# A Hymba layer on one core: segment decays from broadcast loads, a skip term taken before the scan, and another set of PSUM banks in attention

## The chip, the cores and the metric

The kernel runs one layer of a Hymba-style hybrid decoder on one core of a Trainium2 chip. The metric is the device time of one execution in microseconds (us), as the median of repeated runs. All data is float32.

## The reference, cut to what matters

A layer takes 1024 tokens and 16 learned meta tokens ahead of them (L = 1040 positions, model width 1024). One input projection feeds two mixers that stand side by side: a state-space mixer (SSD, 16 heads of 64 in two groups) and a stick-breaking attention (16 heads of 64). Their outputs go through one output projection, and a gated FFN with a short convolution follows. The change touches the two mixers:

```python
# SSD: chunks of 128 positions; the 16 meta tokens are a chunk of their own
xbc = silu(causal_dwconv(xbc, conv_w, conv_b))          # gives xs, Bm, Cm
dt  = softplus(dt_raw + dt_bias);  A = -exp(a_log)
Acs = cumsum(dt * A, axis=-1)                           # within a chunk, for each head
seg = Acs[..., :, None] - Acs[..., None, :]
Ldec = where(causal, exp(where(causal, seg, 0.0)), 0.0) # "segment decays"
CB  = einsum('bclgn,bcsgn->bgcls', Cc, Bc)
y_diag = einsum('bgcls,bgjcls,bcsgjp->bclgjp', CB, Ldec, Xdt)
states = einsum('bclgn,bgjcl,bclgjp->bcgjpn', Bc, exp(Acs[..., -1:] - Acs), Xdt)
# prev = states carried from chunk to chunk
y = y_diag + einsum('bclgn,bcgjpn,bgjcl->bclgjp', Cc, prev, exp(Acs))
y = y + xs * d_skip[:, None]                            # the "D term"
y = rms_norm(y.reshape(B, L, 1024) * silu(z), norm_g)

# stick-breaking attention, 128 queries at a time, strictly causal
zlog = q @ k.T / sqrt(64)
log_beta = log_sigmoid(zlog)
log_keep = where(valid, log_beta - zlog, 0.0)
after = cumsum(log_keep, reverse=True) - log_keep
o = where(valid, exp(log_beta + after), 0.0) @ v
```

## The kernel before

Products that need float32 accuracy are split: a number is held as a high and a low part in a type that TensorE (PE) multiplies faster, and hi·hi + lo·hi + hi·lo are added up in PSUM. VectorE is DVE, ScalarE is ACT, GpSimd is POOL, SyncE is SP; SP issues nearly all DMAs, in program order. PSUM has eight banks of 128 x 512 float32.

The program runs through these stages, one after the other (times in the profiled execution):

- **Head and projections, 0 to 448 us.** Norm, transposes, then the projections. Each feature block of `x` gets its convolution and silu on DVE and ACT (`conv_acts`, L485 to L510), is turned to tokens on PE and stored to DRAM as `xsd`; `dt_acts` (L605 to L668) makes dt, its hi and lo parts and three tables of decays, together six planes of `dtk`. The queries and keys of head pairs 0 to 3 are made here and stored to DRAM (`qkd`).
- **Scan, 448 to 621 us.** 18 units (group g, chunk c), L1021 to L1048; the two units of chunk 0 have 16 positions, the other 16 have 128. `chunk_weights` (L926) of the next unit is written ahead of `chunk_outputs` (L964) and `chunk_store` (L997) of this one. A unit makes the decays of its eight heads: ACT scales the triangle `tri` by dt·A's hi part eight times (`sgh`, L938), POOL does the lo part in one operation (`sgl`, L940), PE sums each along its columns (`sg`, four matmuls 512 wide, L947), ACT takes the exponential out of PSUM (`em`, L949). DVE multiplies by C·B (`cbm`, `em`, L953, L954). POOL makes `xdt` = x·dt (L957) and `yo` = x·D (L960). PE makes what the carried state gives (`yf`, L975), DVE scales it (`yt`, L977), POOL adds it to `yo` (L979). DVE makes `xw` (L983), PE the chunk's new state (`st`, L986), POOL and DVE the carried one (`pv`, L991, L994). PE gathers y in features by tokens: eight products of `em` and `xdt` (L1005), then `yo` added through a transpose (L1008). DVE multiplies by the gate (`zk`, L1012), ACT squares it (`sqk`, L1016).
- **Attention, 621 to 1032 us.** 8 head pairs p, each with 8 blocks i of 128 queries (`block_weights`, L1083): PE makes the logits `z` of up to three chunks of keys (L1101, two banks of PSUM to a tile, two tiles), ACT two sigmoids of each (`kp`, `bt`, L1102, L1103), DVE a reversed running product (`kp`, L1106), POOL the weights (`bt`, L1108). Some blocks later PE turns them to keys by queries (`tw`, L1120, in the same two tiles as `z`), ACT copies them out (`th`, L1122), and PE multiplies by v (`av`, L1135).
- **Rest of the first half of the output projection to 1079 us, its second half to 1172 us, FFN to 1831 us.** The change leaves these as they are, but for the size of the steps in which the output projection is handed out.

What sets the order. The projections of head pairs 4 to 7 (`pj_q`, `pj_k`: 32 chains of 24 matmuls of 246 or 260 columns) are not made ahead: they are **fill**, handed out in half chains by the generator `qk_fill` (L858) to keep PE at work in the scan and in attention; after them come the output projection's chains (`mo`, `out_steps`, L1283). A chain owns one of the two banks `mm` from its first matmul until ACT and DVE have taken it out (`st`, L864, L865). `SCAN_FILL` gives the half chains that go to the scan (30, and 4 ahead of it); the rest go to attention, the same number to each block (L1352, L1357). In attention the order of PE is the order in which the code is written (`pe_order`); the other engines, and PE in the scan, are ordered by a scheduler. `turn` is attention's queue: the transposes of a block begin once more than two blocks wait in it (L1367).

```python
        for p in range(8):                                  # L1356
            for i in range(NT):
                block = block_weights(p, i); next(block, None)   # z of two chunks of keys
                if mix: block_mix(*mix.pop(0))                   # av of an older block
                do(before)                                       # fill
                run(block)                                       # third chunk, then kp and bt
                if len(turn) > 2: ahead = begin_turn()           # tw and th of an older block
```

## Time and profile before

| what | value |
|---|---|
| median of 3 runs (lowest to highest) | 1831.24 us (1830.93 to 1832.59) |
| the profiled execution | 1833.03 us |
| its span, first to last instruction | 1831.3 us |
| TensorE clock granted, mean over the span | 0.974 of full speed |
| matmuls / all instructions | 11550 / 29209 |
| moved by DMA | 230.89 MB, 126 GB/s on average |

The page of the profile gives each engine's busy time and its share of the span, then the span in 40 slices in which a digit is the busy share in tenths; `PEclk` is the granted clock in the same way. A row of a window view gives, for a stretch of the span, its length, the busy time and number of instructions of PE, of PE's weight loads (PEld) and of the other engines, then the granted clock, the busy share of the DMA engines and their rate. A row of a view of groups gives line, engine, operation, output and inputs, shape, count, then the busy time, the mean of one in ns, and the engine's idle time just ahead of such instructions with what ended it. A row of a view of waits reads: who waited for whom, us in total, times, the longest.

### The profile page before, as it was taken

How to read it: one execution, taken by the hardware profiler on the slowest of the kernel's cores; microseconds unless marked ns; L12 is line 12 of the kernel's file. 1: busy time of each engine (PE TensorE's matmuls, PEld its weight loads, DVE VectorE, ACT ScalarE, POOL GpSimd, SP SyncE). 2: the span in 40 equal slices, each digit the busy share in tenths (PEclk: the TensorE clock that was granted, in tenths of full speed). 3: DMA queues.
4: the chain of work that ended last, by engine and by line, in shares of the span. 5: the costliest groups of instructions: out<-in, count | busy, mean ns of one | idle time of the engine just before them, and what ended most of it. 6: DMA issues, size and time to landing. Idle time of an engine off the chain costs nothing. (4 is left out here: it accounts for less than half of the span.)

```text
span 1831.3 us, 29209 instructions
## 1 busy us (share of the span) xinstructions
PE 1700.7 (93%) x11550; PEld 1465.1 (80%) x11550; DVE 1126.4 (62%) x1177; ACT 837.3 (46%) x1378; POOL 975.3 (53%) x687
## 2 busy tenths in 40 slices
PE   6899999999888888887789999999999999999998
PEld 5899999977666677675567778899889999888887
DVE  7755642453477666668555137766666666657777
ACT  6433333321455466676666334543333333334544
POOL 3655766321788677578667311267677677600001
PEclk9999999999799999998999999999999999999999
DMA  5233224335664332334211274323223333187335
GB/s 209 78 112 103 82 93 162 129 128 183 189 201 125 118 101 92 123 101 136 69 54 54 86 241 166 131 80 116 87 87 109 104 104 108 60 284 246 102 98 190
DMA packets 123144, 230.89 MB, mean 126 GB/s; under 512 B 13472, under 2 KB 55992, under 8 KB 122368
## 3 DMA queue, kind: packets, MB, share of 16 engines
q1 hardware_dynamic: 123008, 229.03, 38.4%
q8 instruction: 91, 1.49, 0.4%
q14 instruction: 45, 0.37, 0.1%
HBM read 151.31 MB, written 77.14 MB: 125 GB/s over the span
## 5 line engine op out<-in xcount | busy, mean ns | idle before, releaser
L1106 DVE TENSOR_TENSOR_SCAN kp<-kp,hold 128x272 f32<-128x272 f32 (+7 forms) x128 | 212.6, 1706 | 106.1 <-ACT kp L1102 32.3
L1108 POOL TENSOR_TENSOR bt<-bt,kp 128x256 f32<-128x256 f32 (+7 forms) x128 | 212.5, 1679 | 103.8 <-DVE kp L1106 89.5
L179 POOL TENSOR_TENSOR wlo<-wr,whi 128x1024 fp32r<-128x1024 f32 x43 | 99.3, 2318 | 40.3 <-ACT whi L178 40.3
L2093 POOL TENSOR_TENSOR fms<-fms 128x1 f32<-128x1 f32 x8 | 2.3, 289 | 221.9 <-ACT dh L1978 195.6
L1101 PE MATMUL z<-qk,qk 64*128 64x328 f32 (+8 forms) x672 | 80.7, 356 | 41.3 <-ACT th L1122 35.3
L1101 PEld LDWEIGHTS z<-qk,qk 64*128 64x128 f32 x672 | 52.9, 192 | 64.4 <-ACT th L1122 49.4
L1122 ACT ACTIVATE th<-tw 128x1024 f32<-128x1024 f32 (+2 forms) x96 | 75.2, 820 | 56.0 <-PE tw L1120 43.6
L1102 ACT ACTIVATE kp<-z 128x288 f32<-128x288 f32 (+6 forms) x112 | 83.0, 741 | 31.9 <-POOL cb L1109 17.7
L178 ACT ACTIVATE whi<-wr 128x1024 fp32r<-128x1024 f32 x43 | 45.7, 1064 | 110.9 <-PE fX L1644 67.5
L1120 PE MATMUL tw<-ident,bt 128*128 128x128 f32 x576 | 79.8, 281 | 15.5 <-ACT bt L1103 12.6
L1978 ACT ACTIVATE dh<-ar 128x512 fp32r<-128x512 f32 x77 | 48.7, 633 | 94.3 <-PE dnB L2056 44.7
L1716 DVE SCALAR_TENSOR_TENSOR ga<-gr,pp,ga 128x1024 f32<-128x1024 f32 x44 | 69.2, 1572 | 34.4 <-ACT ga L1709 33.6
L1120 PEld LDWEIGHTS tw<-ident,bt 128*128 128x128 f32 x576 | 65.4, 144 | 30.9 <-ACT bt L1103 15.6
L1135 PE MATMUL av<-th,v 128*64 128x128 f32 x1152 | 83.0, 292 | 0.3 <-ACT th L1122 0.3
L1103 ACT ACTIVATE bt<-z 128x288 f32<-128x288 f32 (+6 forms) x112 | 83.3, 743 | 0.0
L1979 DVE TENSOR_TENSOR dl<-ar,dh 128x512 fp32r<-128x512 f32 x77 | 53.2, 691 | 47.1 <-ACT dh L1978 47.1
L1135 PEld LDWEIGHTS av<-th,v 128*64 128x64 f32 x1152 | 66.6, 145 | 14.5 <-issue 12.1
L1777 POOL TENSOR_TENSOR al<-wr,ah 128x512 fp32r<-128x512 f32 x20 | 28.7, 1433 | 76.9 <-ACT ah L1776 76.8
L2056 PE MATMUL dnA<-dl,dh 128*128 128x512 f32 x176 | 68.5, 389 | 0.0
L2056 PE MATMUL dnA<-dh 128*128 128x512 f32 x176 | 68.5, 389 | 0.0
L2056 PE MATMUL dnA<-dh,dl 128*128 128x512 f32 x176 | 68.5, 389 | 0.0
L2056 PE MATMUL dnB<-dh 128*128 128x512 f32 x132 | 51.3, 389 | 0.0
(989 smaller groups left out, 6244.7 us busy)
## 6 DMA issues: line engine op xcount, KB each, us to landing
wr<-in_w_up SPq DMA_DIRECT2D x44, 512.0 KB
fds<-ga SPq DMA_DIRECT2D x44, 256.0 KB
b<-in_w_down SPq DMA_DIRECT2D x44, 256.0 KB
ar<-fds SPq DMA_DIRECT2D x44, 256.0 KB
fda<-ga SPq DMA_DIRECT2D x33, 256.0 KB
ar<-fda SPq DMA_DIRECT2D x33, 256.0 KB
qk<-qkd SPq DMA_DIRECT2D x16, 520.0 KB
qk<-qkd SPq DMA_DIRECT2D x16, 513.0 KB
```

The lines of the kernel that those rows point to most:

```text
L179: nc.gpsimd.tensor_tensor(l, raw, h.bitcast(F32), op=ALU.subtract)
L1101: mm(z[:, j, :w], u[h, :], r[h, a:a + w], start=s_ == 0, stop=s_ == 2)
L1102: nc.scalar.activation(kp[:, :, a:a + w], z[:, :, :w], AF.Sigmoid, scale=-QSCALE)
L1103: nc.scalar.activation(bt[:, :, a:a + w], z[:, :, :w], AF.Sigmoid, scale=QSCALE)
L1106: nc.vector.tensor_tensor_scan(kp[:, j][:, ::-1], kp[:, j][:, ::-1], hold[:, L - n:L][:, ::-1], 0.0, op0=ALU.mult, op1=ALU.max)
L1108: nc.gpsimd.tensor_tensor(bt[:, j, 0:m], bt[:, j, 0:m], kp[:, j, 1:m + 1], op=ALU.mult)
L1120: nc.tensor.transpose(tw[:, j, b, :], bt[:, j, c0:c0 + P], ident)
L1122: copied[0] = nc.scalar.activation(th[:, :, :nb, :], tw[:, :, :nb, :], AF.Copy).ins
L1135: mm(av[halves[j], :], v[:, kb, halves[j]], th[:, j, b, :], start=kb == 0, stop=kb == i)
L1716: nc.vector.scalar_tensor_tensor(v, self.g[jj][:, :, i:i + 256], fconv_w[:, j, i:i + 1], v, op0=ALU.mult, op1=ALU.add)
L1979: sub(lo[:, k], raw, hi[:, k].bitcast(F32), op=ALU.subtract)
L2056: mm(banks[BANK[n], t], u[:, 0, c], v[:, 1, :], start=(n in (1, 2, 5) and p == 0 and i == 0), stop=(p == NPR - 1 and i == 2), skip_group_c ...
```

## The change

In words, part by part:

1. **Segment decays.** `decay(0)` also copies the cumulative sums out of PSUM into `dtk[1]` (dt·A's hi and lo planes go; `dtk` has five planes). `turn_acs` turns them on PE (rows are chunk and head, columns positions), ACT copies them out and two DMAs store them to DRAM as `acsd`. Each unit loads its eight rows of 512 bytes to all 128 partitions (`load_bc`, 512 KB, two buffers, issued two units ahead). ACT makes relu(Acs[l] − row) eight times and one exponential of 128x1024 with scale −1. `sgh`, `sgl`, `sg` and `lowr` go.
2. **Multiplying by C·B** is cut in two: DVE takes six of the eight heads, POOL two.
3. **D term.** In the projection stage ACT scales each of the eight x blocks by D (128x1040) and SP stores it (`xdd`, 520 KB each). In the scan a unit loads 256 KB of it (`xd`); DVE adds it to y after PE, ahead of the gate. `yo` goes: both POOL operations, and the wait of the transposes for the second; they take `yt` from DVE.
4. **`xw`** moves from DVE to POOL.
5. **Fill.** Chains are handed out in quarters (6 matmuls). `SCAN_FILL` 30 becomes 36 half chains, and 8 half chains' worth of quarters is counted ahead of the scan where 4 half chains were, which are the same matmuls; so 6 half chains more are in the scan and 6 fewer in attention. In attention the rest is shared by the block's number in its pair (`FILL_AT`), few to the short blocks and more to the long ones, and in pieces between `z`, `av`, `tw`.
6. **Attention.** `zz` tiles 2 become 3 (six banks); the bank of `tp` goes, its users take a `zz` tile; `mm` has one bank in attention, two again behind it. `kp` buffers 2 become 3, `bt` 3 become 4, the queue begins its transposes one block later. k is loaded as one tile, q by blocks of 128 KB three blocks ahead; `qkd` holds both parts in one tensor.
7. **Output projection** steps are quarters too; `mo` is the same work.

```diff
-SCAN_FILL = 30
+SCAN_FILL = 36
+FILL_AT = (1, 1, 1, 4, 5, 6, 6, 6)
 def psum_mm(name):
-        return ps.tile([P, 512], F32, tag="mm", name=name, bufs=2)
+        return ps[0].tile([P, 512], F32, tag="mm", name=name, bufs=ps[1])
 def psum_zz(name):
-        return stage[0][1].tile([P, 2, 512], F32, tag="zz", name=name, bufs=2)
+        return stage[0][1].tile([P, 2, 512], F32, tag="zz", name=name, bufs=3)
 def plain_steps(...):
-                if halves_ and k == KB // 2:
-                    yield
+                if halves_ and k and k % halves_ == 0:
+                    yield 0
 def conv_acts(...):
+        def skip():
+            xd = raw[:, 0:L]
+            nc.scalar.activation(xd, box["d"], AF.Copy, scale=ssd_d[:, b:b + 1])
+            nc.sync.dma_start(out=xdd[b // 4][b % 4], in_=xd)
-        taps_ = [lambda j=j: tap(j) for j in range(4)] + [silu]
+        taps_ = [lambda j=j: tap(j) for j in range(4)] + [silu] + [skip] * (b < 8)
 def chunk_weights(g, c):
-            for h in range(8):
-                nc.scalar.activation(sgh[:nr, h, :nr], tri[:nr, :nr], AF.Copy,
-                                     scale=adh[:nr, c, 8 * g + h:8 * g + h + 1])
-            nc.gpsimd.tensor_tensor(sgl[:nr, :, :nr], tri..., adl..., op=ALU.mult)
-            for j in range(2):
-                pz = psum_z(f"sg{nm}_{j}").rearrange("p (a b) -> p a b", b=P)
-                for i, src in enumerate((sgh, sgl)):
-                    mm(pz[:nr, :, :nr], lowr[:nr, :nr], src[:nr, 4 * j:4 * j + 4, :nr], ...)
-                nc.scalar.activation(em[:nr, 4 * j:4 * j + 4, :nr], pz[:nr, :, :nr], AF.Exp)
+            for h in range(8):
+                nc.scalar.activation(em[:nr, h, :nr], bc[:nr, h, :nr], AF.Relu, scale=-1.0,
+                                     bias=acs[:nr, c, 8 * g + h:8 * g + h + 1])
+            nc.scalar.activation(em[:nr, :, :nr], em[:nr, :, :nr], AF.Exp, scale=-1.0)
...
-            nc.gpsimd.tensor_tensor(yo[:nr], xsc, dskip..., op=ALU.mult)
 def chunk_outputs(...):
+            nc.sync.dma_start(out=xd[:, :, y0:nr], in_=xdd[g][:, :, c0 + y0:c0 + nr]...)
-                nc.gpsimd.tensor_tensor(yo[:nr], yo[:nr], yt[:nr], op=ALU.add)
-                nc.vector.tensor_tensor(xw[:nr], xdt[:nr], dec..., op=ALU.mult)
+                nc.gpsimd.tensor_tensor(xw[:nr], xdt[:nr], dec..., op=ALU.mult)
 def chunk_store(...):
-            nc.vector.tensor_tensor(zk[:, :, ts], tp[:, :, ts], zk[:, :, ts], op=ALU.mult)
+            nc.vector.tensor_tensor(xd[:, :, ts], tp[:, :, ts], xd[:, :, ts], op=ALU.add)
+            nc.vector.tensor_tensor(zk[:, :, ts], xd[:, :, ts], zk[:, :, ts], op=ALU.mult)
 # attention
+    ps[:] = stage[0][1], 1
-        kpt = ap.tile([P, 2, L], F32, tag="kp", name=f"kp{nm}", bufs=2)
-        btt = ap.tile([P, 2, L], F32, tag="bt", name=f"bt{nm}", bufs=3)
+        kpt = ap.tile([P, 2, L], F32, tag="kp", name=f"kp{nm}", bufs=3)
+        btt = ap.tile([P, 2, L], F32, tag="bt", name=f"bt{nm}", bufs=4)
-            do(before)
-            run(block)
-            if len(turn) > 2:
-                ahead = begin_turn()
+        some(2)
+        run(block)
+        some(1)
+        if len(turn) > 3:
+            ahead = begin_turn()
+            some(1)
+        run(ahead)
+        some(9)
```

How the instructions move is seen best at three places. The rows of before and of the changed kernel stand apart; a row gives the line, the operation, the output and the inputs by the program's names, and the shape. First PE in the scan, between two units' pieces of fill (`yt` are the products that gather y and the transposes behind them, `sg` the sums of the segments, `pj_k`, `pj_q` fill):

```order
L215 MATMUL pj_k_1_260_5115<-b12rh,wl_k_4489 128x260
L1005 MATMUL yt_3_5128<-em_3_4991,xdt_3_5005 64x128 x8
L1008 MATMUL yt_3_5128<-ident,yo_3_5007 128x128 x4
L947 MATMUL sg_4_0_5159<-sgh_4_5147,lowr 128x512
L947 MATMUL sg_4_0_5159<-sgl_4_5148,lowr 128x512
L947 MATMUL sg_4_1_5163<-sgh_4_5147,lowr 128x512
L947 MATMUL sg_4_1_5163<-sgl_4_5148,lowr 128x512
L951 MATMUL cb_4_5167<-ct_4444,bt_4443 128x128
L215 MATMUL pj_k_1_260_5115<-b22h,wh_k_4488 128x260
```

The same place of the changed kernel:

```order
L217 MATMUL pj_q_0_0_5066<-b11h,wl_q_4754 128x246
L1024 MATMUL yt_3_5100<-em_3_4962,xdt_3_4978 64x128 x8
L1027 MATMUL yt_3_5100<-ident,yt_3_5079 128x128 x4
L217 MATMUL pj_q_0_0_5066<-b21h,wh_q_4753 128x246
L217 MATMUL pj_q_0_0_5066<-b21l,wh_q_4753 128x246
```

The four `sg` matmuls are gone from between the transposes and the fill, and the transposes take `yt` of DVE where they took `yo` of POOL.

Second, DVE in the scan, one unit (`em` is the multiplication by C·B, `zk` the gate, `xw` the state's input, `pv` the carried state), of before:

```order
L953 TENSOR_TENSOR cbm_3_5002<-cb_3_5000,tri 128x128
L954 TENSOR_TENSOR em_3_4991<-em_3_4991,cbm_3_5002 128x1024
L977 TENSOR_TENSOR yt_2_5013<-yf_2_5011,dtk_4439 128x512
L994 TENSOR_TENSOR pv_2_5020<-st_2_5018,pv_2_5020 128x512
```

and of the changed kernel, with the two operations that end a unit:

```order
L973 TENSOR_TENSOR cbm_4_5148<-cb_4_5146,tri 128x128
L884 TENSOR_TENSOR st_5130<-pj_q_0_0_5066,st_5130 128x246
L975 TENSOR_TENSOR em_4_5136<-em_4_5136,cbm_4_5148 128x768
L998 TENSOR_TENSOR yt_3_5169<-yf_3_5167,dtk_4448 128x512
L1014 TENSOR_TENSOR pv_3_5175<-st_3_5173,pv_3_5175 128x512
L1031 TENSOR_TENSOR xd_3_5165<-yt_3_5184,xd_3_5165 128x512
L1032 TENSOR_TENSOR zk_3_5163<-xd_3_5165,zk_3_5163 128x512
```

`em` of the next unit still stands ahead of `yt` of this one on DVE; it is a quarter shorter, `xd` stands ahead of `zk`, and `xw` is gone from DVE.

Third, PE in attention, where a chain of fill opens (`z` logits, `av` weights times v). Before:

```order
L1101 MATMUL z_4_1_7324<-qk_2_6687,qk_2_6681 128x328 x2
L1135 MATMUL av_1_7338<-th_1_0_7311,v_6847 64x128 x4
L215 MATMUL pj_q_0_260_7344<-b11h,wh_q_6654 128x260
L215 MATMUL pj_q_0_260_7344<-b11l,wh_q_6654 128x260
L215 MATMUL pj_q_0_260_7344<-b11h,wl_q_6655 128x260
```

After, the end of one chain and the start of the next:

```order
L217 MATMUL pj_k_1_260_6691<-b22h,wh_k_5779 128x260
L217 MATMUL pj_k_1_260_6691<-b22l,wh_k_5779 128x260
L217 MATMUL pj_k_1_260_6691<-b22h,wl_k_5780 128x260
L217 MATMUL pj_q_0_0_6801<-b11h,wh_q_6177 128x246
L217 MATMUL pj_q_0_0_6801<-b11l,wh_q_6177 128x246
L217 MATMUL pj_q_0_0_6801<-b11h,wl_q_6178 128x246
```

At this place the second chain opens right behind the first, and both use the one bank `mm`.

More of the change, by code (lines that the diff above doesn't have):

```diff
@@ L1407, in tile_layer @@
     stp_.close()
+    stage[0][0].close()
+    stage[0] = None
+    ps[:] = ctx.enter_context(tc.tile_pool(name="psum2", bufs=2, space=PSUM)), 2
     psum_stage("psC")
```

284 lines of the change are left out of this document (155 added, 129 removed).

## The prediction

> **What bounds the kernel now.** I read the page's first two parts, then the window view by stage, then who PE waits for in the two stages that the change is about.
>
> ```profile
> span 1831.3 us, 29209 instructions
> PE 1700.7 (93%) x11550; PEld 1465.1 (80%) x11550; DVE 1126.4 (62%) x1177; ACT 837.3 (46%) x1378; POOL 975.3 (53%) x687
> 62.00:364.00 302.00, 287.07 (x2329) 283.47 (x2328) 152.46 (x146) 109.72 (x150) 184.77 (x107) 0.98 0.33 110
> 448.00:621.00 173.00, 143.16 (x940) 111.39 (x939) 109.43 (x127) 79.72 (x220) 125.05 (x89) 0.89 0.54 166
> 621.00:1032.00 411.00, 353.01 (x3142) 279.57 (x3141) 255.85 (x210) 270.70 (x445) 292.37 (x224) 0.96 0.28 90
> 1172.00:1831.00 659.00, 653.04 (x3750) 574.87 (x3748) 449.25 (x515) 266.16 (x381) 300.85 (x182) 1.00 0.39 127
> ```
>
> PE is busy for 93% of the span. The FFN (1172 to 1831) leaves it 6 us idle, and the change doesn't enter it. Idle PE is found in two rows: the scan (448 to 621) has 173 − 143.2 = 30 us and a granted clock of 0.89, attention (621 to 1032) 411 − 353 = 58 us and a clock of 0.96. No other engine there is near its stage's length. So the change can win by taking matmuls away, by closing these 88 us, and by the clock that comes with it. The views of PE's waits say whom it waits for, the first three rows in the scan, the other three in attention:
>
> ```profile
> PE yt L1008 <- POOL yo L979: 21.2, 15, 2.9
> PE sg L947 <- ACT sgh L938: 3.8, 1, 3.8
> PE pj_k L215 <- DVE st L865: 3.5, 1, 3.5
> PE z L1101 <- ACT th L1122: 35.3, 45, 4.3
> PE tw L1120 <- ACT bt L1103: 12.6, 12, 4.3
> PE z L1101 <- ACT bt L1103: 5.1, 8, 1.7
> ```
>
> In the scan one wait recurs in 15 units: the transposes want `yo`, POOL's second addition. In attention 35.3 + 12.6 + 5.1 = 53.0 us are waits for ACT to empty a `zz` tile, `z` behind `th` above all: two tiles serve both.
>
> **The scan.** DVE's timeline has the gate, once a unit; these are the first and the last of the 16 full units:
>
> ```profile
> 494.69 0.68 DVE L1012 TENSOR_TENSOR zk<-yt,zk 128x512 f32<-128x512 f32 x1
> ...
> 620.25 0.69 DVE L1012 TENSOR_TENSOR zk<-yt,zk 128x512 f32<-128x512 f32 x1 [3.17 <-PE yt L1008]
> ```
>
> (620.25 − 494.69) / 15 = 8.37 us a unit, after a start of 494.69 − 448 = 47 us. The groups of the stage price what goes and moves:
>
> ```profile
> L938 ACT ACTIVATE sgh<-tri,dtk 128x128 fp32r<-128x128 f32 (+1 forms) x144 | 42.8, 384 | 5.8 <-DMA dtk<-dtkd 4.4 <-PE sg L947 1.3
> L954 DVE TENSOR_TENSOR em<-em,cbm 128x1024 f32<-128x1024 f32 (+1 forms) x18 | 34.5, 1918 | 1.9 <-ACT em L949 0.7
> L940 POOL TENSOR_TENSOR sgl<-tri,dtk 128x1024 fp32r<-128x1024 f32 (+1 forms) x18 | 33.1, 1838 | 20.0 <-PE sg L947 11.1 <-DMA dskip<-in_rows 6.5 <-PE cb L951 2.2
> L979 POOL TENSOR_TENSOR yo<-yo,yt 128x512 f32<-128x512 f32 x16 | 23.0, 1436 | 20.3 <-DVE yt L977 20.3
> L957 POOL TENSOR_TENSOR xdt<-xk,dtk 128x512 f32<-128x512 f32 (+1 forms) x18 | 20.8, 1156 | 0.7 <-DMA xk<-xsd 0.7
> L983 DVE TENSOR_TENSOR xw<-xdt,dtk 128x512 f32<-128x512 f32 (+1 forms) x16 | 20.8, 1300 | 1.8 <-POOL xdt L957 1.8
> L960 POOL TENSOR_TENSOR yo<-xk,dskip 128x512 f32<-128x512 f32 (+1 forms) x18 | 19.2, 1065 | 1.5 <-PE yt L1008 1.5
> L949 ACT ACTIVATE em<-sg 128x512 f32<-128x512 f32 (+1 forms) x36 | 18.9, 552 | 36.1 <-PE sg L947 32.8 <-PE yt L1005 3.1
> L947 PE MATMUL sg<-sgh,lowr 128*128 128x512 f32 (+1 forms) x36 | 15.6, 432 | 3.8 <-ACT sgh L938 3.8
> L977 DVE TENSOR_TENSOR yt<-yf,dtk 128x512 f32<-128x512 f32 x16 | 10.9, 680 | 2.2 <-PE yf L975 2.2
> L1016 ACT ACTIVATE sqk<-zk 128x512 f32<-128x512 f32 (+1 forms) x18 | 10.5, 582 | 35.6 <-DVE zk L1012 35.6
> ```
>
> POOL's 125 us lose `sgl` 33.1 and both `yo` 23.0 + 19.2; they gain `xw` at the price of `xdt`, 16 x 1.16 = 18.5, and two eighths of `em` at half an `xdt`, 18 x 0.58 = 10.4 (256 elements against 512): 79. DVE's 109 lose `xw` 20.8 and a quarter of `em` 8.6 and gain 16 additions `xd` at the gate's 0.69, 11: 91. ACT: eight relu of 128x128 for eight scalings, one exponential for two (18 x 1.10); unchanged at 80, unless reading a loaded row costs it more than reading `tri`. The work of all three falls or stays; none becomes the bound by its sum.
>
> PE, by the timeline of one unit, and DVE's gate behind it:
>
> ```profile
> 535.75 0.36 PE L215 MATMUL pj_q<-b11h,wh_q 128*128 128x246 f32 x1
> ...
> 537.19 0.39 PE L947 MATMUL sg<-sgh,lowr 128*128 128x512 f32 x1
> ...
> 538.11 0.38 PE L951 MATMUL cb<-ct,bt 128*128 128x128 f32 x2
> 538.33 1.02 PE L975 MATMUL yf<-pv,ct 128*128 128x512 f32 x2
> 539.19 1.02 PE L986 MATMUL st<-xw,bn 128*128 128x512 f32 x2
> 541.52 1.09 PE L1005 MATMUL yt<-em,xdt 128*64 128x128 f32 x16
> 545.18 0.66 PE L1008 MATMUL yt<-ident,yo 128*128 128x128 f32 x4 [2.57 <-POOL yo L979]
> ```
>
> ```profile
> 545.88 0.69 DVE L1012 TENSOR_TENSOR zk<-yt,zk 128x512 f32<-128x512 f32 x1 [1.55 <-PE yt L1008]
> ```
>
> By the starts, 12 fill matmuls take 537.19 − 535.75 = 1.44 us (0.12 each) and four `sg` 538.11 − 537.19 = 0.92, which go: 16.6 us of PE in 18 units. Back come six half chains, 72 x 0.12 = 8.6 us, taken from attention. A unit of PE is then 24 fill matmuls (2.9), `cb` 0.2, `yf` and `st` 0.86 each, `yt` 1.1, transposes 0.5: 6.4 us.
>
> With POOL out of the path, what is late next is the ring DVE–ACT–DVE–PE. DVE has `em` of the next unit ahead of `yt` of this one, so a unit's transposes wait for: `xd` 0.69, `zk` 0.69, `sqk` 0.58, the last relu 0.38, exponential 1.10, `em` on DVE 0.75 x 1.92 = 1.44, `yt` 0.68, transposes 0.66; 6.2 us, plus eight hand-overs of about 0.1 (transposes of 545.18 + 0.66 and the gate behind them at 545.88 are the near end), 7.0. I take 7.1, above PE's 6.4. 15 x (8.37 − 7.1) = 19 us, and 5 of the 47 us of start (the 3.8 us wait for `sgh` and half of a `yo` wait for each of the first units): **−24 us**. Bounds: PE's own sum, 143 − 16.6 + 8.6 = 135 us, would be −38, with the clock at 1.0 −44; nothing gained is 0.
>
> This hides new transfers: `bc` 16 x 512 KB and `xd` 16 x 256 KB, 12.6 MB. The stage moved 166 GB/s at a DMA share of 0.54, so 307 GB/s at a full share: 41 us on top of 0.54 x 173 = 93, 134 of 149 us. That is tight. They are issued one to two units ahead (7 to 14 us); if late, each unit waits and the gain is gone.
>
> **A rule against the split of `em`.** The row of `em` (1918 ns mean) and `yo` against `xdt` on POOL, 1436 against 1156 ns for as many elements, show that DVE and POOL slow each other or differ by operand; the rows can't part the two. The Trainium skill, "SBUF — State Buffer", section "Who interferes with whom", says that a DVE instruction with two SBUF inputs and a GpSimd instruction that reads SBUF exclude each other, and that the later one waits for the whole of the other. The longer means fit it; no row shows a full block. As a mechanism of this kernel: the two parts of `em` run one after the other, 1.44 + 0.58 where the ring has 1.44, and the scan gains 16 x 0.58 = 9 us less: 1778 instead of 1768.
>
> **Attention.** Three things, against 411 us.
>
> - *Waits.* With three `zz` tiles `z` no longer needs the tile that `th` is emptying; the third `kp` and the deeper queue let a block run ahead. Of 53.0 us I take three fifths, **−32**. Bounds: 0 and −53. Not all, since ACT's row says that its order binds as well, and POOL has 292 us of work that must still fit:
>
> ```profile
> ACT kp L1102 <- POOL cb L1109: 17.7, 12, 3.4
> ```
>
> - *Fill and clock.* The 72 matmuls that went to the scan: **−9**. The clock drops behind long waits, here six `z` matmuls ahead of and behind a gap of 3.72 us:
>
> ```profile
> 824.38 0.80 PE L1101 MATMUL z<-qk,qk 64*128 64x392 f32 x6
> 828.90 1.35 PE L1101 MATMUL z<-qk,qk 64*128 64x392 f32 x6 [3.72 <-ACT th L1122]
> ```
>
> With half the long gaps gone the clock's 0.96 becomes 0.98: 353 x 0.02 = **−7** (0 to −14, all the way to 1.00). The Trainium skill, "TensorE: Matmul & The Clock Gate", section "What's actually happening", has the array at half clock after an idle window of some 3.4 us; these rows agree (1.35 against 0.80). By that rule, if every gap fell below it, the whole of the 14 would come.
>
> - *One `mm` bank.* A chain now opens only when ACT and DVE have taken the last one out. Some 21 chains open in attention (85 quarters of four to a chain); at five places the next stands right behind the last. The nearest row is the 3.5 us of `pj_k` behind DVE's `st`. Five such are about 17; fill, `z` and queue slack lie ahead of the others, and PE gets most of it back from waits it would have had: **+6** (0 to +90, below).
>
> Sum −42, with bounds of −76 (53 + 9 + 14) and above zero by the last point.
>
> **Projections.** Eight ACT operations of 128x1040, priced by
>
> ```profile
> L498 ACT ACTIVATE cdX<-cdX 128x1040 f32<-128x1040 f32 x8 | 8.6, 1077 | 46.3 <-DVE cdX L494 28.3 <-issue 18.0
> ```
>
> are 8.6 us more for ACT, which is busy for 110 of 302 us, so they fit beside PE; a PSUM bank that ACT empties later, two transposes and their copies remain: **+3** (0 to 9, all of it exposed). Eight stores of 520 KB, 4.3 MB, go into a DMA share of 0.33. Loading q by blocks and in one tile moves the same bytes: 0.
>
> **Sum.** −24 − 42 + 3 = −63. The profiled execution took 1833.03 us, 1.8 above the median of 1831.24; on the median's scale 1831.2 − 63 = **1768 us**.
>
> **Rivals.**
>
> 1. *The scan's unit does not get shorter* (late `bc` or `xd`). The start's 5 us stay, 19 go: 1768 + 19 = 1787. For it: the DMA share near 0.9. Against: loads two units ahead. Its milder form has DVE and POOL exclude each other on `em`: 1778, as above; for it the longer means, against it that POOL is idle for half the stage and may come before or behind.
> 2. *Attention gains its fill alone*: `z` waits for ACT elsewhere, since ACT's work (271 of 411 us) is the same. Then 32 + 7 go, less the 6: 1768 + 33 = 1801. For it: all three wait rows name ACT. Against: `th` with 35.3 us is a wait for a tile, which there is one more of.
> 3. *Slower: the single `mm` bank.* DVE's `st` stands in line with the products along keys (`kp`, two to a block):
>
> ```profile
> L1106 DVE TENSOR_TENSOR_SCAN kp<-kp,hold 128x272 f32<-128x272 f32 (+7 forms) x128 | 212.6, 1706 | 106.1 <-ACT kp L1102 32.3
> ```
>
> Where two stand ahead, an opening waits 2 x 1.71 + 0.8 (copy and subtraction) = 4.2 us, and PE's order is fixed, so all behind it waits. 21 x 4.2 = 88, 82 beyond my 6: 1850. It makes the kernel slower from (63 + 6) / 21 = 3.3 us an opening. For it: five openings are adjacent; against: the other 16 have blocks between.
> 4. *The change does not do what it says*: PE has the same idle time, only `sg` leaves. 1831 − 16.6 + 3 = 1818.
>
> **How the numbers follow.** Forecast 0.53, `em` in turn (1778) 0.10, rival 1 0.11, rival 2 0.11, rival 3 0.08, rival 4 0.07. The range leaves out rival 3, most of rival 4 and the far end of the bounds (−44 − 76): 1736 to 1810. A measurement can tell about 0.2% from no change, 3.7 us. Faster by more: all but rival 3 and mixtures of 3 with the rest, 0.87; within 0.05; slower 0.08.
>
> **What would show it.** In the scan: no wait of the transposes for POOL, gates 7.1 us apart, clock over 0.93, the stage near 149 us; a unit still near 8.4 with PE waiting for `xd` or `em` is rival 1. In attention: waits of `z` behind `th` near 10 us, the stage near 369 us; waits of `pj` or `mo` behind DVE's `st` of 4 us at every opening are rival 3. The projections within 3 us of 302. What would make it wrong: a stage that the change does not enter, the FFN above all, getting longer.

## The result, and the profile after

The changed kernel takes **1840.2 us** (median of 6 runs, 1838.4 to 1850.3) beside 1831.1 (1825.9 to 1832.6): 0.63% slower, ratio 1.0063 with a 95% interval of 1.0038 to 1.0087. The forecast was 1768, and "slower" had a chance of 0.08. The profiled execution took 1840.4.

First the page of the changed kernel, its first two parts:

```profile
span 1838.7 us, 29152 instructions
PE 1693.4 (92%) x11472; PEld 1464.7 (80%) x11472; DVE 1112.2 (60%) x1178; ACT 844.8 (46%) x1370; POOL 925.9 (50%) x669
```

The work of three engines did fall (PE 7 us, DVE 14, POOL 49; ACT's rose by 7), and the span rose by 7.4 us. Where, a window view with the boundaries at the same events of both kernels says: last sums of the projections, last v product, first `z`, last product of attention's edges, last halo product of the first output half, first FFN product. Four rows of before, whose stages end at other times than those of the forecast's table, and the same four after:

```profile
62.00:363.50 301.50, 287.07 (x2329) 283.47 (x2328) 151.96 (x146) 109.72 (x150) 184.77 (x107) 0.98 0.33 110
448.60:621.50 172.90, 143.06 (x940) 111.26 (x939) 109.43 (x127) 80.00 (x220) 125.05 (x89) 0.89 0.54 166
621.50:1043.80 422.30, 364.31 (x3190) 288.17 (x3189) 256.61 (x212) 272.36 (x448) 294.77 (x225) 0.96 0.28 89
1076.10:1225.20 149.10, 149.09 (x806) 128.34 (x805) 98.18 (x103) 68.52 (x106) 38.56 (x48) 1.00 0.43 142
```

```profile
62.00:372.10 310.10, 290.30 (x2333) 286.00 (x2331) 152.67 (x145) 118.95 (x160) 181.72 (x107) 0.97 0.36 120
458.10:627.20 169.10, 131.49 (x933) 105.58 (x931) 97.62 (x134) 82.63 (x207) 87.41 (x74) 0.88 0.77 241
627.20:1045.30 418.10, 365.77 (x3140) 293.15 (x3140) 256.51 (x207) 268.36 (x443) 286.80 (x224) 0.94 0.31 92
1075.00:1231.60 156.60, 150.48 (x797) 127.79 (x794) 97.53 (x103) 68.54 (x106) 38.68 (x48) 0.98 0.41 136
```

Projections +8.6 us, scan −3.8 (forecast −24), attention −4.2 (forecast −42), the output projection from its first half's end on +7.5, where nothing was forecast; with −2.6 ahead of that, +0.9 in v and +1.0 in the FFN that is the 7.4. In the scan the engines' sums came near those worked out (DVE 98 for 91, POOL 87 for 79, PE 131 for 135), yet PE is idle for 38 us where it was 30. In attention PE's idle time (the length less PE's busy time) fell from 58.0 to 52.3 us only, and PE is busy as long as before, at a clock of 0.94. The 72 fill matmuls have left the stage, but 23 wider products of the output projection (`mo`, 288 where there were 265) have come in from the stage behind it.

PE's waits of the changed kernel, in the projections, the scan, attention and the output projection:

```profile
PE tt_X L479 <- ACT xtkX L485: 5.7, 4, 1.7
PE tt_X L484 <- ACT xtkX L485: 4.6, 4, 1.2
...
PE yt L1027 <- DVE yt L998: 22.7, 6, 9.8
PE st L1006 <- POOL xw L1003: 5.8, 2, 5.4
...
PE av L1165 <- ACT th L1152: 10.2, 16, 2.8
PE z L1131 <- ACT bt L1133: 9.5, 4, 5.3
PE pj_k L217 <- DVE st L884: 9.0, 3, 4.3
PE pj_q L217 <- DVE st L884: 7.8, 3, 5.4
PE avc L1185 <- DVE thc L1177: 5.3, 7, 0.8
PE z L1131 <- DVE st L884: 3.8, 1, 3.8
PE mo L1322 <- ACT ma L1335: 3.7, 4, 1.2
PE z L1131 <- ACT th L1152: 2.6, 8, 0.7
PE halo L1285 <- DVE st L884: 2.5, 1, 2.5
...
PE mo L1322 <- DVE mb L1844: 6.1, 5, 3.8
```

The waits that the change was aimed at are gone: no transpose waits for POOL, and of the 53.0 us of `z` and `tw` 12 are left. Others stand in their place: in the scan six waits for `yt` instead of 15, but of up to 9.8 us; in attention 19 us of waits for DVE's `st` (9.0 + 7.8 + 2.5), which are seven openings of the one bank, and 15 for `th` and `thc`; between scan and attention 3.8 us, in which the first `z` waits for DVE's `st` of the scan's last chain of fill; behind attention `mo` for `mb`.

In the scan the gates (`zk`) are 6.8 us apart on average, but for two gaps of 13.4 and 16.7. The second, on DVE, ACT and SP (SP rows are DMA issues):

```profile
593.64 0.69 DVE L1032 TENSOR_TENSOR zk<-xd,zk 128x512 f32<-128x512 f32 x1
...
604.87 0.41 DVE L884 TENSOR_TENSOR st<-pj_q,st 128x246 fp32r<-128x246 f32 x1 [9.99 <-ACT st L883]
605.21 2.62 DVE L975 TENSOR_TENSOR em<-em,cbm 128x768 f32<-128x768 f32 x1
...
610.35 0.69 DVE L1032 TENSOR_TENSOR zk<-xd,zk 128x512 f32<-128x512 f32 x1
```

```profile
595.32 1.06 ACT L969 ACTIVATE em<-em 128x1024 f32<-128x1024 f32 x1
603.52 1.06 ACT L191 ACTIVATE wh_q<-wr_q 128x1024 fp32r<-128x1024 f32 x1 [7.15 <-DMA wr_q<-in_w_q]
604.48 0.36 ACT L883 ACTIVATE st<-pj_q 128x246 fp32r<-128x246 f32 x1
604.74 2.14 ACT L967 ACTIVATE em<-bc,dtk 128x128 f32<-128x128 f32 x7
```

```profile
589.64 0.50 SPq L906 DMA_DIRECT2D k<-qkd  x1
...
591.32 0.98 SPq L953 DMA_DIRECT2D bc<-acsd  x1
596.39 0.37 SPq L990 DMA_DIRECT2D zk<-zd  x1
...
598.53 0.59 SPq L190 DMA_DIRECT2D wr_q<-in_w_q  x1
```

ACT stands for 7 us at the head of its queue for a weight block of the fill; the chain's `st` and the next unit's relus are behind it, DVE waits for ACT, PE for DVE. The first gap has the same chain: ACT stands 3.7 us for `wr_q`, to 538.21, DVE then 5.3 for ACT's `st`, PE 5.0 for `yt`. The second weight load was issued late, since SP stood still from 592 to 596, and behind 1 MB of k and 512 KB of `bc`. The DMA engines' share in that stretch is 0.95, by a window row of it; the stage's is 0.77 where it was 0.54:

```profile
590.00:606.00 16.00, 6.81 (x58) 5.23 (x53) 5.56 (x10) 6.62 (x17) 4.79 (x4) 0.89 0.95 299
```

In the kernel before, this load leaves SP long before ACT uses it. The first of the two in the scan:

```profile
490.19 0.50 SPq L188 DMA_DIRECT2D wr_q<-in_w_q  x1
...
532.64 1.06 ACT L189 ACTIVATE wh_q<-wr_q 128x1024 fp32r<-128x1024 f32 x1
```

That is 42 us ahead, and the second leaves 74 us ahead (540.65 for 614.76). In the changed kernel the two leave 4.5 and 5.0 us ahead (533.71 for 538.21, 598.53 for 603.52), the first just ahead of the end of ACT's other work (534.5), the second 2 us behind it (596.4).

### The profile page after: what moved, and what is told of

Read it like the earlier page. It is cut to its first block, busy times and chain, and to the rows that moved or that the text cites. A ratio compares the mean times of both kernels' runs of the same rounds, so it can differ in the third digit from the quotient of the medians.

```text
span 1838.7 us, 29152 instructions
## 1 busy us (share of the span) xinstructions
PE 1693.4 (92%) x11472; PEld 1464.7 (80%) x11472; DVE 1112.2 (60%) x1178; ACT 844.8 (46%) x1370; POOL 925.9 (50%) x669
## 5 line engine op out<-in xcount | busy, mean ns | idle before, releaser
L1131 PE MATMUL z<-k,q 64*128 64x328 f32 (+8 forms) x672 | 79.3, 361 | 16.9 <-ACT bt L1133 9.5
L1165 PE MATMUL av<-th,v 128*64 128x128 f32 x1152 | 79.6, 284 | 10.6 <-ACT th L1152 10.2
L1165 PEld LDWEIGHTS av<-th,v 128*64 128x64 f32 x1152 | 63.7, 140 | 26.5 <-ACT th L1152 19.8
L1131 PEld LDWEIGHTS z<-k,q 64*128 64x128 f32 x672 | 56.8, 202 | 33.4 <-ACT bt L1133 11.1
L1322 PE MATMUL mo<-wohb,yh 128*128 128x512 f32 x128 | 52.0, 406 | 6.1 <-DVE mb L1844 6.1
```

What stands on the lines that cost most here:

```text
L1131: mm(z[:, j, :w], u[h, :], r[h, a:a + w], start=s_ == 0, stop=s_ == 2)
L1165: mm(av[halves[j], :], v[:, kb, halves[j]], th[:, j, b, :], start=kb == 0, stop=kb == i)
L1322: recent[0] = mm(acc, u[:, k, :], v[:, cs], start=(k == 0 and j == 0), stop=(k == 7 and j == 2))
```

## The experiments

Each kernel is the changed one with an edit; from e5 on all have e1's edit too. "Share" is the fill by blocks. Lengths of stages in us, each from a window view of one profiled execution (PR projections, SC scan, AT attention, O1 what is left of the output projection's first half, O2 from there to the FFN), and the median time beside that of before in the same runs:

| kernel | PR | SC | AT | O1 | O2 | time | before |
|---|---|---|---|---|---|---|---|
| before | 301.5 | 172.9 | 422.3 | 32.3 | 149.1 | | 1831.1 |
| changed | 310.1 | 169.1 | 418.1 | 29.7 | 156.6 | 1840.2 | 1831.1 |
| e1 whole chain | 311.1 | 169.9 | 418.4 | 29.9 | **146.4** | 1831.5 | 1831.5 |
| e2 two `mm`, two `zz` | 309.2 | 168.3 | **433.1** | 30.0 | 155.3 | 1855.2 | 1831.5 |
| e3 `bc` loaded once | 313.4 | **148.8** | 418.1 | 29.9 | 155.3 | 1821.4 | 1831.5 |
| e4 scaling late | **334.1** | 168.1 | 417.1 | 29.9 | 156.5 | 1861.5 | 1831.5 |
| e5 bank freed by ACT | 313.7 | 166.1 | **408.5** | 29.9 | 146.3 | 1817.1 | 1830.1 |
| e6 even share | 310.1 | **159.8** | **412.8** | 30.0 | 146.3 | 1815.0 | 1830.1 |
| e7 queue of before | 306.6 | 168.5 | **405.7** | 31.5 | 150.5 | 1824.8 | 1830.1 |
| e8 scaling on POOL | 311.6 | 170.5 | 417.3 | 29.8 | 146.4 | 1831.1 | 1830.1 |
| e9 late splitting | 312.6 | 174.2 | 417.6 | 29.8 | 146.4 | 1832.7 | 1831.8 |
| e10 no scaling, no store | **300.3** | 168.6 | 417.5 | 30.0 | 146.4 | 1821.9 | 1831.8 |
| e11 e5 + e6 + e7 + e9 | 310.8 | 158.4 | **399.4** | 31.3 | 150.8 | 1806.3 | 1831.8 |
| e12 e5 + e7 + e9 | 311.2 | 167.6 | 412.4 | 31.5 | 150.5 | 1823.5 | 1831.8 |
| e13 third `zk`, `xd` | 311.6 | 166.3 | 418.9 | 29.8 | 146.4 | 1828.0 | 1831.1 |
| e14 scaling in place | **303.1** | 169.3 | 420.6 | 29.9 | 146.4 | 1821.5 | 1831.1 |
| e15 no store | 306.4 | 169.0 | 419.1 | 29.9 | 146.4 | 1832.0 | 1831.1 |
| e16 e5 + e6 + e7 + e13 + e14 | 303.1 | 163.4 | 401.9 | 31.2 | 150.5 | 1803.3 | 1831.1 |
| e17 k loads late | 316.8 | **162.5** | 420.4 | 30.0 | 146.4 | 1826.9 | 1829.3 |
| e18 e16 + e17 | 302.6 | **156.0** | 399.7 | 31.2 | 150.5 | 1796.3 | 1829.3 |

Where the projections' code is untouched their length lies between 306.6 and 316.8 us; below that the table's differences there mean little. PE's idle time in that stage is steadier: 19.5 to 19.9 us in these kernels, twelve with the changed one. Where the edit leaves the scan's code alone, the scan lies between 168 and 171, but for e6, of which more below.

**e1, the size of a step.**

```diff
-        run(steps, 2)      # second half of the output projection, first call for a token block
+        run(steps, 4)
```

> The changed kernel with one number different: in the second half of the output projection a token block starts with four steps (a whole chain, as before) where the change left two (quarters now, so half a chain). Theory: the step's size is why this stage is 93 us where it was 86: the stage from 1086 us goes back to 86 to 87 us, PE's waits of mo for DVE's mb fall from 6.1 us to under 1, and the whole is 6 us shorter (about 1834). Rival (the reopened PSUM pool or the later end of attention is the cause): no change, 1840.

O2 went from 156.6 to 146.4 us, the total to 1831.5 (1.0008, 0.9994 to 1.0023):

```profile
1075.80:1222.20 146.40, 146.40 (x793) 126.06 (x794) 98.15 (x103) 67.95 (x106) 38.63 (x48) 1.00 0.42 145
```

PE has no idle time left there. The theory held, by more than it said. The line is not in the diff: `out_steps` now yields after a quarter of a chain, and this caller, which asked for two steps, got half of what it had. The evacuation `mb` of the token block's first chain then stood behind the norm's work on DVE, and the second bank came late.

**e2, the banks.**

```diff
-  ... tag="zz", name=name, bufs=3)        ps[:] = stage[0][1], 1
+  ... tag="zz", name=name, bufs=2)        ps[:] = stage[0][1], 2
```

> The changed kernel with PSUM shared out as before in attention: two mm banks, two zz tiles. Theory (the single mm bank ate the gain): the waits of pj, z, halo and mo for DVE's st or ACT's ma, 27 us, go below 5, waits of z behind th come back by less, since the queue is deeper, and attention is 10 to 20 us shorter than 418 (total 1820 to 1830). Rival (the third zz tile was worth what the bank costs, and the clock or the thin fill in short blocks keeps the stage long): z waits come back by 25 us or more, total 1837 to 1855.

The theory fell: attention is 15 us longer, total 1.0135 of before (1.0109 to 1.0160). The waits for `st` went, and those for the tiles came back:

```profile
PE z L1131 <- ACT th L1152: 25.3, 42, 2.9
PE tw L1150 <- ACT bt L1133: 13.0, 7, 5.5
PE z L1131 <- ACT bt L1133: 11.3, 9, 1.5
```

Before, the same banks gave 422.3, with 72 fill matmuls more (9 us) and 23 of `mo` fewer (5 us, at the 0.24 that e7 shows below). So in this order of work the third tile is worth more than the bank, and something else in the change costs attention some 14 us.

**e5, the one bank, freed sooner.**

```diff
                 nc.scalar.activation(st[:, 0, :m], acc[:, :m], AF.Copy)
-                nc.vector.tensor_tensor(st[:, 1, :m], acc[:, :m], st[:, 0, :m]..., op=ALU.subtract)
+                nc.scalar.activation(full, acc[:, :m], AF.Copy)          # full = st[:, 1, :m] as f32
+                nc.vector.tensor_tensor(st[:, 1, :m], full, st[:, 0, :m]..., op=ALU.subtract)
```

> The changed kernel with the repaired step of e1 (1831.5 us) and a chain's bank emptied by ACT alone: ACT copies the high part and the whole sum out of PSUM, DVE subtracts in SBUF. One mm bank and three zz tiles stay. Theory (openings wait in the one bank for DVE's st behind the products along keys): the 24 us of waits of pj, z and halo for DVE's st fall below 8, and attention falls from 418 to about 402 to 406. Rival (these waits only stand where PE would wait for z, tw or th anyway, as two banks with two zz tiles suggest): attention within 4 us of 418, with waits of z for ACT and av for th instead.

Attention 408.5, 10 us shorter; total 0.9932 of before (0.9909 to 0.9956). The waits for DVE's `st` are gone, and 3.1 us for ACT's are left; about half of what went came back as other waits (`av` for `th` from 10.2 to 15.5).

**e6, the share; e7, the queue.**

```diff
-FILL_AT = (1, 1, 1, 4, 5, 6, 6, 6)         # e6
+FILL_AT = (1, 1, 1, 1, 1, 1, 1, 1)
-        if len(turn) > 3:                  # e7
+        if len(turn) > 2:
```

> The changed kernel with the repaired step of e1 and the fill shared evenly, as before, among the eight blocks of a pair. Theory (the thin fill of the short blocks leaves PE idle and the heavy fill of the long ones comes where DVE and POOL set the pace anyway): attention shorter than 418 by 6 to 15 us. Rival (the uneven share does what it is for): attention longer by 5 us or more.

> The changed kernel with the repaired step of e1 and the queue of before (transposes begin when more than two blocks wait). Theory (a third zz tile, not the deeper queue, took the z waits away): attention within 4 us of 418. Rival 1 (the depth is what hides DVE and POOL): attention 8 us or more longer, waits of tw for POOL's bt appear. Rival 2 (the depth costs, since it holds bt and the zz tiles longer): attention 4 us or more shorter.

The even share gives attention 6 us and the scan 10: its second long unit was 12 us and not 17. There the weight load left SP at 585.94, ahead of the k load (592.48); in the changed kernel it left behind it (598.53 and 589.64). Why the share of a later stage moves these loads is open. Total 0.9918 (0.9897 to 0.9939). The old queue gives 12.7 us in attention, of which 6 come back as output projection that is left for later (264 products of `mo` instead of 288; O1 +1.6, O2 +4.1 against e1, 0.24 us for each): a net of 7. The medians say the same (1824.8 against 1831.5), though the ten executions of e7 spread from 1818.2, the profiled one, to 1830.6. PE's idle time in attention fell by 5.7 us (54.8 to 49.1). So the depth costs; rival 2 held. The waits of `tw` for POOL's `bt` that rival 1 named are 1.3 us.

**e11, e12, together.**

> The changed kernel with the repaired step of e1, the bank emptied by ACT alone (e5), the queue of before (e7), the even share of fill (e6) and the late splitting of weights (e9). If the losses are apart from one another, attention falls by 10, 13 and 6 us from 418, to about 390, and the scan to about 154: total about 1785. If two of them are the same wait seen twice, attention stops at 400 to 405: total 1798 to 1805.

> As e11_all_even, but with the changed kernel's uneven share of fill. If the uneven share itself costs PE time in attention, this is 4 us or more slower than e11; if its cost came only with the deeper queue or the bank, the two agree within 3 us.

Attention 399.4 with the even share and 412.4 without. Against e1's 418.4 the sum of e5, e6 and e7 would be 28 us, they give 19: partly the same waits. The share alone is 13 us here, which is an upper reading: the profiled execution of e12 is the longest of its ten (1829.5), and nearly all of the 13 is PE's busy time (352.0 and 364.2 us for 3116 matmuls each, at clocks of 0.95 and 0.92), not its idle time (47.4 and 48.1). e11 is at 0.9868 of before (0.9843 to 0.9892). The scan's 154 of the expectation was not seen, since e9 failed.

**e3, the broadcast loads.**

```diff
+            if c > 1:                       # the rows of the group's first full chunk again
+                bcs[g, c] = kept[g]
+                return
```

> The changed kernel without the broadcast loads from the second full chunk on: later units read the rows of their group's first full chunk again, so the decays of later chunks are left out of the output; 14 loads of 512 KB (7.3 MB) go. Theory (the two long units of 13.4 and 16.7 us are DMA queues: ACT waits at the head of its queue for a weight load): the waits of ACT wh_q for wr_q (10.9 us) fall below 3, both long units come to 7 to 9 us, the scan is 12 to 17 us shorter than 169 (total 1824 to 1829). Rival (the units are long for DVE and POOL getting in each other's way): under 4 us shorter.

The scan is 148.8 us, 20 shorter; no unit is over 9.6 us, and ACT has no wait for `wr_q`. That the long units come with the broadcast loads is shown, and that DVE and POOL in each other's way do not make them alone, since their work is the same here. That the volume makes them is not: the two weight loads of e3 also left SP 10 and 38 us ahead of ACT's use (511.89 for 521.52, 540.93 for 579.08).

```profile
460.30:609.10 148.80, 128.19 (x933) 103.19 (x931) 93.91 (x134) 82.26 (x207) 85.69 (x74) 0.91 0.72 225
```

**e9, e13, e17: by which way.** e9 writes the splitting of a weight block 10 quarters later, e13 gives `zk` and `xd` three buffers, e17 holds two k loads back:

```diff
+            if col is not None:             # e17: k of pair 0 waits for chunk 6, of pair 1 for the last
+                nc.vector.tensor_copy(k[:, 0, 0:1], sq[:, col:col + 1])
             nc.sync.dma_start(out=k.bitcast(F32), in_=qkd[p][1])
```

> The changed kernel with the repaired step of e1; a weight block's load is issued where it was, but ACT's and POOL's splitting of it is written 10 quarters later, shortly ahead of its first use. Theory (the two long units of the scan, 13.5 and 17 us, are ACT standing at the head of its queue for a weight load that the fuller DMA queues bring late, with everything else of ACT behind it): ACT's waits for wr_q vanish, both units come to 7 to 9 us, the scan falls from 169 to 152 to 156 us, total 1815 to 1820. Rival (the transfers themselves are too many, xd, bc and zk are late then): the long units only move or stay above 11 us, the scan within 6 us of 169.

> The changed kernel with the repaired step of e1 and a third buffer for zk and for xd. Theory (SP stands at the head of its queue until a store of zk has landed and its buffer is free, so the weight load behind it starts late and ACT waits for that): SP's waits of the zk load for yd (23 us) fall below 5, the long units (13.5 and 17 us) come to 7 to 9 us, the scan falls from 169 to 150 to 156 us. Rival (the transfers are simply too many for that stretch): the long units stay above 11 us, the scan within 5 us of 169.

> The changed kernel with the repaired step of e1; the loads of k for the first two head pairs (1 MB each), which ran in the middle of the scan, are held back by a one-column write that needs the squares of chunk 6 and of the last chunk. Theory (the long units are a stretch in which the DMA engines have more to move than they can: a k load, two weight blocks and the unit's own loads at once): the second long unit falls from 17 us to 7 to 10, the first from 13.5 to 8 to 11, the scan from 169 to 155 to 161 with a DMA share as high as before. Rival (something other than the volume of that stretch, such as one wait on SP or ACT, makes the long units): both stay over 12 us.

e9 changed nothing to the good (gaps of 14.1 and 20.5): ACT waited 15.2 us for `wr_q`, since the scheduler put the load as late as the splitting. e13 left them too (11.6 and 19.5), and SP's waits of `zk` for `yd` stayed at 26 us, so a third buffer is not what they lack. e17 took away the second gap (9.4 at most there), not the first (13.3), where one wait of ACT for `wr_q` is left (3.0 us). The scan is 162.5. So the k load in that stretch is a part of the cause. With it held back the scheduler also issued the second weight load five units sooner, 28 us ahead of its use:

```profile
595.95 1.04 ACT L191 ACTIVATE wh_q<-wr_q 128x1024 fp32r<-128x1024 f32 x1
```

The load left at 567.78, and ACT doesn't wait. The traces of all the kernels agree on this: a `wr_q` load of the scan that left SP 4.1 to 7.4 us ahead of ACT's use was waited for each time, 34 times in all, and one that left 9.6 us or more ahead never (both in before and in e3, the second in e17 and in e18). In e17 and e18 the broadcast loads were all there. This speaks for the load's place in SP's queue more than for the volume; moving that load alone was not tried.

**e4, e8, e10, e14, e15: the scaling by D.**

```diff
-        taps_ = [tap ...] + [silu] + [skip] * (b < 8);  turns = [turn_(0), turn_(1), turn_(2)]
+        taps_ = [tap ...] + [silu];  turns = [turn_(0), turn_(1), turn_(2)] + [skip] * (b < 8)   # e4, e14
-            xd = raw[:, 0:L]
+            xd = box["d"]                                                                       # e14
```

e8 has the operation on POOL at its old place, e15 leaves out the stores, e10 the operations and the stores.

> The changed kernel with each scaling by D moved behind the last of the three turns of its block, so that ACT's copies of the turned blocks no longer stand behind it. Theory (the projections' 8.6 us are PE waiting for these copies): waits of tt_X for xtkX and cdX go from 11.3 back to about 6 us, the projections from 310 to 304, the total falls by 4 to 7 us. Rival (ACT's added work or the 4.3 MB of stores cost it wherever they stand): no change beyond 2 us.

> The changed kernel with the repaired step of e1 and the scaling by D done by POOL at the same place of the program; the buffers are held as in the changed kernel. Theory (ACT's copies of the turned blocks stand behind the scaling): waits of tt_X go from 11.3 to about 6 us and the projections from 310 to 303 to 306. Rival (buffers of the raw rows held until the stores have landed): no change, or longer, since POOL takes longer than ACT for it.

> The changed kernel with the repaired step of e1 and without the scaling by D and its stores; the scan loads the gate's rows in their place, so the D term is left out. Theory (the scaling, by any engine, keeps a raw row and with it the next steps back): the projections fall from 310 to 301 to 304 us, waits of tt_X from 11 to 6. Rival (the half clock after waits, which differ from run to run, or the turned sums and their copies cost it): the projections stay at 308 or more.

> The changed kernel with the repaired step of e1; the scaling by D is done by ACT in place in the block's own tile, behind its three turns, and stored from there, so the raw row is free as early as before. Theory (a raw row is held until its scaled copy has landed in DRAM, and PE's next sums wait for it): the projections fall from 310 to 301 to 304 us. Rival (the eight operations or stores cost it, wherever they stand): 308 or more.

> The changed kernel with the repaired step of e1 and without the eight stores of the scaled rows (the scaling stays; the scan loads the gate's rows in their place, so the D term is left out). Theory (the raw row is held by the store, not by the scaling): the projections fall from 310 to about 302 to 304. Rival (the scaling stands in ACT's line ahead of the copies of the turned blocks): 308 or more, with tt_X still waiting 10 us or more for xtkX.

Without the scaling and its stores the projections take 300.3 us, in place behind the turns 303.1: the scaling's place and buffer cost 7 to 10 us, not its work, which e14 keeps. PE's idle time says it more sharply. It is 14.4 us before, 14.5 in e10 and 14.4 in e14, but 19.8 in the changed kernel, 19.5 in e15 and 20.4 in e8. So 5.4 of the 8.6 us come from the scaling's place ahead of the turns or from the buffer that it takes there, whichever engine does it and with or without the store; the rest is PE's busy time, which for the same code varies from 287.1 to 297.0 us with the clock. e4 shows one half of it: with the raw row held to the last turn, sums wait for the stores.

```profile
DVE craw_x L319 <- DMA xdd<-craw_x: 32.1, 2, 16.7
```

In the changed kernel that wait does not show; there it is the copies `xtkX` (10.3 us above; 4.9 in e14, 10.7 in e15, which has the scaling at its old place and no store). e8 speaks against ACT's line as the whole of it: with the scaling on POOL the waits for `xtkX` are 11.6 us. DVE's busy time there rose from 152.7 to 158.1, so POOL's operation had a price of its own. e15 (306.4) lies between its two forecasts in length, and has the rival's waits. The place and the buffer are not told apart.

**e16, e18, all repairs together.**

> All that is to win together: the repaired step of e1, the bank emptied by ACT alone (e5), the even share (e6), the queue of before (e7), the third buffers of e13 and the scaling in place of e14. If these add up as stages: projections 302, scan 152, attention 399, the rest as in e11, about 1790. If e13 and e14 fail, 1806 as e11.

> e16_best (1803) with the k loads of e17. If the long units were volume: the scan falls from 163 to 152 to 156, total 1792 to 1797. If not: 1803 again.

e16: 0.9846 (0.9823 to 0.9869); its scan stayed at 163.4 us and not 152, since e13 failed. e18: **1796.3 us, 0.9831 of before (0.9810 to 0.9851)**, faster than both kernels by 33 and 44 us. Against the changed kernel its projections are 7.5 us shorter, the scan 13, attention 18, the output projection 5. The scan came at the far end of its forecast; no unit there is over 9.6 us.

```profile
449.30:605.30 156.00, 130.87 (x932) 105.23 (x931) 101.68 (x134) 87.15 (x227) 87.13 (x72) 0.89 0.80 254
605.30:1005.00 399.70, 353.04 (x3116) 281.87 (x3116) 275.47 (x210) 269.76 (x454) 304.14 (x225) 0.94 0.32 98
```

## Why the prediction was wrong, point by point

- **What bounds the kernel, and the waits named: right.** POOL's `yo` and the `zz` tiles were where PE waited, and the change removed both.
- **Scan, the ring: near in time, not in mechanism.** 7.1 us a unit was forecast; 13 of 15 took 6.80 on average ((118.5 − 30.1) / 13, from 504.2 to 622.7 without the two long ones). But the ring needs `em` of the next unit ahead of `yt` on DVE, as the order shown ahead of the prediction has it, and in ten of 15 units `yt` comes first:

```profile
555.79 0.68 DVE L998 TENSOR_TENSOR yt<-yf,dtk 128x512 f32<-128x512 f32 x1
556.82 0.96 DVE L975 TENSOR_TENSOR em<-em,cbm 128x768 f32<-128x768 f32 x1 [0.35 <-ACT em L969]
```

  In the seven units from 545.04 to 593.64 PE is busy for 46.74 of 48.60 us, and the other 1.86 are one wait for `yt`. There PE's own work sets 6.9 us a unit, for which the forecast had 6.4. The order with `em` first stands in five units, the two long ones among them, and five of PE's six waits for `yt` are in these. So the agreement in time is partly luck, and so is e3's 148.8 beside the forecast's 149: it is made of 4 us less at the start, 23 less in the units and 3 more behind the last.
- **Scan, "this hides new transfers ... 134 of 149 us. That is tight": the step that failed.** The volume was worked out (41 MB came of it, 0.77 of the stage), but it was set against the stage's mean. The price fell in two stretches, through a transfer that the sum doesn't have: `wr_q`, which now left SP 5 us ahead of its use and stood at the head of ACT's queue. The rival had named `bc` and `xd` as what would be late. `bc` was late too, but cost ACT 6.8 us in five waits, against 10.9 in two for `wr_q`. Also, none of the 5 us of start came: the first full gate stands 46 us behind the stage's beginning, as before (504.2 − 458.1), and behind the last gate the stage is 3 us longer, where the first `z` waits for `st`.
- **Attention, "of 53.0 us I take three fifths, −32": the step that failed.** The step takes a removed wait for time gained. 41 of the 53 us went, more than forecast, but PE's idle time fell by 5.7 us: it stood at `st`, `th` and `thc` instead. With the bank, the queue and the share put right (e11) it is still 47.4 us, where the forecast's terms leave 58 − 32 + 6 = 32, and PE waits in the main for ACT and POOL:

```profile
PE av L1181 <- ACT th L1168: 20.1, 17, 4.2
PE tw L1166 <- POOL bt L1154: 9.6, 6, 3.1
PE z L1147 <- ACT bt L1149: 7.2, 6, 4.2
```

  Rival 2 ("`z` waits for ACT elsewhere") comes nearest to this in mechanism. "One `mm` bank ... +6" was a little low: openings cost 19 us of waits, of which 10 are real (e5). The deeper queue was counted as help; it costs 7 net (e7), and it is what brings the 23 products of `mo` into the stage, some 5 us that the "−9" of fill doesn't have. The share of fill was not priced at all; it costs 6 to 13 (e6, e12 against e11). Rival 3 had the right mechanism at too high a price (seven openings of 21 waited, 2.8 us each and not 4.2), and was not what made the kernel slower by itself: two banks at the price of a tile are 15 us worse (e2).
- **Attention, "0.96 becomes 0.98": wrong way, 0.94.** The long waits did not vanish but moved. Attention opens at a lower clock than before, where it was 1.00. The first row is of before, the other two of the changed kernel:

```profile
621.40:633.40 12.00, 9.64 (x82) 7.82 (x81) 8.84 (x20) 7.65 (x15) 8.49 (x17) 1.00 0.57 162
627.10:639.10 12.00, 11.34 (x78) 9.94 (x78) 9.40 (x22) 7.74 (x14) 10.43 (x18) 0.64 0.80 210
639.10:651.10 12.00, 12.00 (x93) 10.19 (x92) 10.95 (x12) 9.50 (x16) 10.18 (x8) 0.82 0.24 56
```

  By the last two rows 12 x (0.36 + 0.18) = 6.5 us of full clock are lost there.
- **Projections, "+3 (0 to 9)": mis-sized, +8.6, of which 5.4 are idle time of PE.** "They fit beside PE" holds for ACT's sum; the copies behind them and the buffer do not (e10, e14).
- **The output projection, not a term of the sum: +7.5, −2.6 ahead of it.** The quarters were taken for "the same work". They are, but a caller that counts steps got half (e1, 10 us). Without this the changed kernel equals the one before.
- **`em` in turn with POOL (1778):** the units came shorter than that rival had them, and e3 leaves none of the missing gain for it.

## What to carry to other kernels

When the grain of a generator is changed, every caller that counts its steps is part of the change, in the diff or not. Added transfers are to be set against the fullest stretch of the stage, and against what else of the in-order queues stands behind them there, not against the stage's mean; a load that was no part of the change may then leave too late. An average that comes out as forecast does not show the forecast's mechanism: the order of the instructions in the trace does. A freed engine or a removed wait is worth what the next in line leaves of it: waits of 53 us in attention were traded for others, and PE's idle time fell by 6.

## What the runs showed of the hardware that was not expected

The product `em` of 768 elements took 0.94 to 0.97 us in eight of the 16 full units and 2.62 in both long units. In the one shown above POOL had a subtraction of two SBUF operands under way:

```profile
604.65 2.35 POOL L192 TENSOR_TENSOR wl_q<-wr_q,wh_q 128x1024 fp32r<-128x1024 f32 x1 [11.19 <-ACT wh_q L191]
606.96 1.44 POOL L975 TENSOR_TENSOR em<-em,cbm 128x256 f32<-128x256 f32 x1
```

604.65 + 2.35 + 0.95 = 607.95, and DVE's operation ended at 605.21 + 2.62 = 607.83: it did its work after POOL's. The Trainium skill, "SBUF — State Buffer", section "Who interferes with whom", says that of two such instructions the later waits for the whole of the other; this case's trace agrees. What it cost the scan was not tried by itself.

The same code of the projections took from 306.6 to 316.8 us in different kernels, with granted clocks of 0.99 to 0.95 for the stage: differences below that between two single profiles of it say nothing. Nearly all of that spread is PE's busy time (287.1 to 297.0 us for the same matmuls); its idle time stayed within 19.5 to 19.9.
